# Gathered u rows for 32 of 384 dense tokens in a retrieval layer, with 68 chunks in the table stage

## The chip, the core and the metric

The kernel runs on one core of a Trainium2 chip. TensorE (PE in the profile, PEld its weight loads) multiplies matrices, VectorE (DVE) and ScalarE (ACT) work elementwise, GpSimd (POOL) issues the indirect DMAs that gather rows by index, and SyncE (SP) issues the other DMAs. Each engine runs its own instructions in the order in which they were placed, and engines wait for each other by semaphores. The metric is the device time of one execution in microseconds; less is better.

## What is computed

One encoder layer over 512 tokens of 1024 channels: a token mixer (sparse attention and pooling), then a retrieval over 16,384 single-neuron experts. Only the second half is touched:

```python
q = (hx @ w_q).reshape(TOKEN_BLOCK, PEER_HEADS, 2, PEER_HALF)
s = jnp.einsum('nhpd,hpkd->nhpk', q, sub_keys)
top_s, top_i = lax.top_k(s, PEER_TOPK)
cand = top_s[:, :, 0, :, None] + top_s[:, :, 1, None, :]
best_s, best_p = lax.top_k(cand.reshape(...), PEER_TOPK)
expert = (i1 * N_KEYS + i2).reshape(TOKEN_BLOCK, PEER_HEADS * PEER_TOPK)   # 128 per token
gate = softmax(best_s)
act = gelu(einsum('nd,ned->ne', hx, u[expert]))
return einsum('ne,ned->nd', gate * act, v[expert])
```

Each token picks 128 experts (8 heads, 16 each). Its activation with an expert is the dot product of the token with that expert's row of `u`, and the output is the sum of the experts' rows of `v`, each times gate and gelu of the activation.

## The kernel before

The 512 tokens go two ways. The last 128 are **sparse**: `sparse()` gathers, for k of 0 to 127, the row of `u` of each token's k-th expert into a 128x1024 tile (`ur`, one indirect DMA on POOL), VectorE multiplies it with the tokens (`hx`) and sums along the row (line 732, one instruction of 1024 elements a partition and a short one that reads the sum), and later the same is done with rows of `v` (`vr`, line 738, added into `sacc` in line 743).

The first 384 tokens (`ND`) are **dense**: all 16,384 experts are computed, in 128 chunks of 128 experts. A chunk has two parts. *Activations*: the 512 KB block `uT[c]` is loaded by `fetch` and split into a high and a low float32r part (ScalarE line 533 `uhe`, VectorE line 534 `ule`); 24 matmuls (8 slices of 128 channels, three products each, lines 570 to 572 or 554 to 556, tile `pse`) give 128 experts x 384 tokens, and ScalarE's gelu stores them (`gelu`). *Contraction*: the activations are multiplied by the gates of the chunk (`gated`, line 781), split again (`Wh`, `Wl`, lines 794, 796), a 512 KB block of `v` is loaded and split (`vh`, `vl`, lines 795, 797), and 18 matmuls of 512 columns (line 805, `acc`) add into six PSUM banks that stay for all 128 chunks.

The gates are wanted as a full table, experts x tokens, since most are zero. `gates(tb)` builds it for one block of 128 tokens: for every token two one-hot matrices (`on`, line 652: which second key; `oa`, line 658: which first key, times the gate, once for each of two float16 parts of the gate), and TensorE multiplies them (line 665, `gm`, two matmuls a token). ScalarE moves the result to `st`, and SP writes it to HBM (`gd`), from where the contraction reads it back in pieces (`g`).

Two stages follow from that:
- **Table stage.** While the tables are built and the keys of the next block are selected (`ProductKeys`), `dense_acts` computes activations of the first KEPT + SPILL = 37 + 22 = 59 chunks, KEPT of them held in SBUF, SPILL written to HBM (`ad`). Program order interleaves them: `act_until` advances the activations in step with the table (fractions `FILL`), and a scheduler then places each engine's instructions.
- **Contraction stage.** A loop over all 128 chunks, in an order written by hand for PE, DVE and ACT. An iteration c forms the weights of chunk c + 1 and the gated values of c + 2, takes some steps of `sparse()` (EARLY = 0.8 in the first SPILL iterations, RATE = 3.0 in those that still compute activations, and `late`, worked out so that all 256 are done 7 chunks before the end), then computes the activations of chunk c + KEPT (the last 69 chunks) or loads spilled ones, and contracts chunk c.

The buffers `up` (of the split `u`), `v`, `vh`, `vl`, `Wh`, `Wl` are two deep each, the gathered rows of `sparse()` five deep.

## Time and profile before

| | us |
|---|---|
| median of 3 runs (lowest, highest) | 1550.58 (1547.45, 1550.72) |
| profiled execution, its own time | 1549.25 |
| span of its instructions | 1547.4 |
| table stage: first dense activations to first `acc` matmul | 405 to 729.5 |
| contraction stage: first `acc` matmul to last | 729.5 to 1541.3 |
| last additions and the write of the output | to 1547.4 |

The time before 405 us (token mixer, query projection) has the same work in both kernels. A row of the timeline gives the start, then the duration of an instruction or of several merged (x2); instructions of one engine overlap by some ten ns, so that what one costs in a row of its kind is the difference of two starts, and that is used below.

### The profile page before, as it was taken

The numbers are of one execution on the slowest core, as the hardware profiler recorded it, in microseconds if no ns is written. First come the engines' busy times: TensorE is split into PE (matmuls) and PEld (weight loads), VectorE is DVE, ScalarE is ACT, GpSimd is POOL, SyncE is SP. The second block draws the span as 40 slices with busy tenths as digits, with TensorE's granted clock in tenths as the row PEclk, the third lists the DMA queues.
The fourth block names the chain that finished last, engine by engine and source line by source line (L and its number), as shares of the span: only waits on it lengthen the run. The fifth ranks groups of instructions, "written<-read, shape, count | busy, mean of one in ns | idle before, by whom it ended". The sixth has DMA issues, their size and how long they took to land.

```text
span 1547.4 us, 22248 instructions
## 1 busy us (share of the span) xinstructions
PE 1504.0 (97%) x7889; PEld 1302.0 (84%) x7889; DVE 1295.0 (84%) x2672; ACT 650.9 (42%) x999; POOL 324.9 (21%) x318
## 2 busy tenths in 40 slices
PE   5899999998999999999999999999999999999998
PEld 3678777886898989899888999999999999998886
DVE  7799886758999899994778888888888888888887
ACT  4643555534445454454334333333333333333332
POOL 0000000000000000001113444444444444453320
PEclk8999999999999999999999999999999999999999
DMA  8422663433236666779989999999999999998883
GB/s 313 163 69 83 213 221 116 157 112 121 78 113 189 193 198 183 224 244 319 330 316 365 323 352 357 318 363 315 359 343 337 355 320 361 328 355 315 314 305 145
DMA packets 158545, 393.91 MB, mean 255 GB/s; under 512 B 13537, under 2 KB 68449, under 8 KB 158306
## 3 DMA queue, kind: packets, MB, share of 16 engines
q1 hardware_dynamic: 121570, 258.26, 47.8%
q0 software_dynamic: 36864, 134.23, 24.5%
q8 instruction: 62, 1.02, 0.3%
q14 instruction: 49, 0.40, 0.1%
HBM read 358.75 MB, written 33.69 MB: 254 GB/s over the span
## 4 chain that ended last, share of the span: by engine, by line
PE 87%; DVE 8%; DMA 2%; ACT 2%; issue 1%; SPq 0%; ACTq 0%; DVEq 0%
PE acc L805 32%; PE pse L556 6%; PE pse L555 6%; PE pse L554 6%; PE pse L570 4%; PE pse L572 4%; PE pse L571 4%; PE gm L665 3%; PE po L469 1%; DVE ule L534 1%; PE psga L171 1%; PE psga L172 1%; PE psga L173 1%; PE pso L171 1%; PE psgp L171 1%; PE psgp L173 1%
## 5 line engine op out<-in xcount | busy, mean ns | idle before, releaser
L730 POOL DMA_INDIRECT ur<-u,ei x128 | 157.0, 1226 | 601.5 <-DMA ad<-gelu 365.5
L805 PE MATMUL acc<-vh,Wl 128*128 128x512 f32 x768 | 237.3, 390 | 0.0
L805 PE MATMUL acc<-vl,Wh 128*128 128x512 f32 x768 | 237.0, 389 | 0.3 <-DVE vl L797 0.3
L805 PE MATMUL acc<-vh,Wh 128*128 128x512 f32 x768 | 236.7, 389 | 0.0
L738 POOL DMA_INDIRECT vr<-v,ei x128 | 165.0, 1289 | 213.9 <-DVE sacc L743 185.2
L797 DVE TENSOR_TENSOR vl<-v,vh 128x1024 fp32r<-128x1024 f32 x128 | 156.8, 1225 | 57.7 <-ACT vh L795 57.4
L556 PE MATMUL pse<-h2h,ule 128*128 128x384 f32 x552 | 185.2, 336 | 0.1
L555 PE MATMUL pse<-h2l,uhe 128*128 128x384 f32 x552 | 184.7, 335 | 0.0
L554 PE MATMUL pse<-h2h,uhe 128*128 128x384 f32 x552 | 184.4, 334 | 0.0
L794 ACT ACTIVATE Wh<-gelu 128x384 fp32r<-128x384 f32 x106 | 55.6, 525 | 290.9 <-PE acc L805 187.9
L534 DVE TENSOR_TENSOR ule<-ue,uhe 128x1024 fp32r<-128x1024 f32 x128 | 155.9, 1218 | 17.8 <-ACT uhe L533 17.7
L805 PEld LDWEIGHTS acc<-vl,Wh 128*128 128x128 f32 x768 | 144.0, 188 | 30.8 <-DVE vl L797 0.9
L805 PEld LDWEIGHTS acc<-vh,Wl 128*128 128x128 f32 x768 | 144.2, 188 | 29.9
L570 PE MATMUL pse<-h2h,uhe 128*128 128x384 f32 x472 | 168.2, 356 | 0.0
L572 PE MATMUL pse<-h2h,ule 128*128 128x384 f32 x472 | 161.4, 342 | 5.1 <-DVE ule L534 5.1
L743 DVE SCALAR_TENSOR_TENSOR sacc<-vr,wt,sacc 128x1024 f32<-128x1024 f32 x127 | 162.8, 1282 | 2.6 <-DMA vr<-v,ei 0.2
L805 PEld LDWEIGHTS acc<-vh,Wh 128*128 128x128 f32 x768 | 143.2, 188 | 24.5
L533 ACT ACTIVATE uhe<-ue 128x1024 fp32r<-128x1024 f32 x128 | 134.6, 1051 | 60.7 <-PE pse L571 51.1
L571 PE MATMUL pse<-h2l,uhe 128*128 128x384 f32 x472 | 159.5, 338 | 0.0
L732 DVE SCALAR_TENSOR_TENSOR ur<-ur,hx 128x1024 f32<-128x1024 f32 x128 | 150.8, 1220 | 1.6 <-DMA ur<-u,ei 1.5
L795 ACT ACTIVATE vh<-v 128x1024 fp32r<-128x1024 f32 x128 | 135.9, 1061 | 10.0 <-DMA v<-v 9.5
L796 DVE TENSOR_TENSOR Wl<-gelu,Wh 128x384 fp32r<-128x384 f32 x106 | 59.2, 559 | 56.8 <-ACT Wh L794 56.6
(424 smaller groups left out, 2722.0 us busy)
## 6 DMA issues: line engine op xcount, KB each, us to landing
ue<-uT SPq DMA_DIRECT2D x128, 512.0 KB, 5.4
v<-v SPq DMA_DIRECT2D x128, 512.0 KB, 5.7
wada<-w_ada SPq DMA_DIRECT2D x48, 512.0 KB, 4.5
gd<-st SPq DMA_DIRECT2D x24, 1024.0 KB, 5.7
g<-gd SPq DMA_DIRECT2D x48, 512.0 KB, 7.5
ad<-gelu SPq DMA_DIRECT2D x22, 192.0 KB, 3.0
wgp<-w_in SPq DMA_DIRECT2D x8, 512.0 KB, 3.7
wga<-w_in SPq DMA_DIRECT2D x8, 512.0 KB, 3.9
```

Source lines behind the costliest of these rows:

```text
L534: V.tensor_tensor(lo, src, hi.bitcast(F32), op=ALU.subtract)
L554: T.matmul(p, hi[:, k, :], h2h[:, k, :n], start=(k == 0), stop=False)
L555: T.matmul(p, hi[:, k, :], h2l[:, k, :n], start=False, stop=False)
L556: T.matmul(p, lo[:, k, :], h2h[:, k, :n], start=False, stop=(k == DT - 1))
L570: T.matmul(ps, hi[:, k, :], h2h[:, k, :ND], start=(k == 0), stop=False)
L571: T.matmul(ps, hi[:, k, :], h2l[:, k, :ND], start=False, stop=False)
L572: T.matmul(ps, lo[:, k, :], h2h[:, k, :ND], start=False, stop=(k == DT - 1))
L730: G.indirect_dma_start(out=ur, out_offset=None, in_=u, in_offset=bass.IndirectOffsetOnAxis(ap=ei3[:, k:k + 1], axis=0))
L738: G.indirect_dma_start(out=vr, out_offset=None, in_=v, in_offset=bass.IndirectOffsetOnAxis(ap=ei3[:, k:k + 1], axis=0))
L743: V.scalar_tensor_tensor(sacc, vr, wt[:, k:k + 1], sacc, op0=ALU.mult, op1=ALU.add)
L797: V.tensor_tensor(vl, vr, vh.bitcast(F32), op=ALU.subtract)
L805: T.matmul(acc[tb][i], x[:, t], y[:, i * 512:(i + 1) * 512], start=(c == 0 and n == 0), stop=(c == NEXP - 1 and n == 2))
```

## The change

The first 32 of the dense tokens (`US`) no longer take their activations from the chunks. Their 128 experts each are gathered: 32 indirect DMAs of `u`, each of which serves 4 experts of 32 tokens (`UG` = 4 groups on the 128 partitions), each followed by one multiply-and-sum on VectorE (`gathers`). The gelu of these, times the gates, goes through the one-hot products in place of the gate alone (`values`, then `build`), in three bfloat16 parts, so the table holds finished weights for these 32 tokens, and the contraction takes them from the table (`first`).

The activation matmuls have 352 columns in place of 384. The table is built in four segments: tokens 32 to 127 of block 0, blocks 1 and 2, then tokens 0 to 31 of block 0, which must wait for all gathers. HOLD, SPILL, EARLY and RATE are set anew: the table stage has 35 + 33 = 68 chunks, the contraction stage 60, and `late` is 1.714 rows an iteration in place of 1.11.

```diff
-HOLD = 38
-SPILL = 22
+US = 32
+NU = ND - US
+UG = P // US
+HOLD = 36
+SPILL = 33
-EARLY = 0.8
+EARLY = 1.0
-RATE = 3.0
+RATE = 2.95
-FILL = (0.36, 0.72, 1.0)
+SEGS = [(0, US, P, 0.30, 0.4), (1, 0, P, 0.64, 0.4), (2, 0, P, 0.93, 0.4), (0, 0, US, 1.0, 0.0)]
...
-                T.matmul(ps, hi[:, k, :], h2h[:, k, :ND], start=(k == 0), stop=False)
+                T.matmul(ps, hi[:, k, :], h2h[:, k, US:ND], start=(k == 0), stop=False)
...
+        def values():
+            zero = oh.tile([P, P], F32, tag="gs", name="uz", bufs=1)
+            V.memset(zero, 0.0)
+            for i in range(UG):
+                r = slice(i * US, (i + 1) * US)
+                A.activation(zero[r, r], uact[r], AF.Gelu)
+            ps = ptr.tile([P, 4, P], F32, tag="tr", name="uw")[:, 0, :US]
+            T.matmul(ps, zero, con[:, K_SEL:K_SEL + US], start=True, stop=True)
+            V.tensor_tensor(ugate, ps, ugate, op=ALU.mult)
+            part = oh.tile([P, 3, US], BF16, tag="part", name="upart", bufs=1)
+            for i in range(3):
+                A.copy(part[:, i, :], ugate)
+                if i < 2:
+                    V.tensor_tensor(ugate, ugate, part[:, i, :], op=ALU.subtract)
+            yield from build(0, 0, US, ukeys, ulow, [part[:, i, :] for i in range(3)], BF16, 1.0)
...
-                    for i in range(2):
-                        x = oh.tile([P, NA, 4, KL, 2], F16, tag=f"oa{i}", name=f"oa{i}_{tb}_{t}")
+                    for i in range(len(parts)):
+                        x = oh.tile([P, NA, 4, KL, 2], dt, tag=f"oa{i % 2}", name=f"oa{i}_{tb}_{t}")
...
+        def gathers():
+            x = tokens(0, US, "u")
+            e = oh.tile([P, P], F32, tag="gs", name="ue", bufs=1)[:US]
+            V.scalar_tensor_tensor(e, sel[0][0][:US], 128.0, sel[0][1][:US], op0=ALU.mult, op1=ALU.add)
+            for i in range(UG):
+                V.tensor_copy(uei[i * US:(i + 1) * US, :], e[:, i * US:(i + 1) * US])
+            yield
+            for k in range(US):
+                ur = us.tile([P, D], F32, tag="row", name=f"uu{k}", bufs=2)
+                G.indirect_dma_start(out=ur, out_offset=None, in_=u,
+                                     in_offset=bass.IndirectOffsetOnAxis(ap=uei[:, k:k + 1], axis=0))
+                V.scalar_tensor_tensor(ur, ur, 1.0, x, op0=ALU.mult, op1=ALU.mult, accum_out=uact[:, k:k + 1])
+                yield
...
+        first = gts[c // GJ][:, :US // GT, c % GJ, :]
+        groups = lambda x: x[:, :US].rearrange("p (g t) -> p g t", t=GT)
+        A.activation(groups(wh), first, AF.Copy)
+        A.activation(wh[:, US:], w, AF.Copy)
         A.activation(vh, vr, AF.Copy)
-        V.tensor_tensor(wl, w, wh.bitcast(F32), op=ALU.subtract)
+        V.tensor_tensor(groups(wl), first, groups(wh).bitcast(F32), op=ALU.subtract)
+        V.tensor_tensor(wl[:, US:], w, wh[:, US:].bitcast(F32), op=ALU.subtract)
```

VectorE in the table stage, some three quarters through block 2 (`on`, `oa` are the one-hot tiles, `ule` the split of a chunk, `best`, `pos` and `cand` the selection of keys, `uu` a gathered row). Before:

```order
L652 TENSOR_TENSOR on_2_80_7039<-irep,keys_6426 128x1024
L658 TENSOR_TENSOR oa_2_80_7041<-gt_2_4_6915,rest_4_6911 128x1024
L658 TENSOR_TENSOR oa_2_80_7043<-gt_2_4_6917,rest_4_6911 128x1024
L908 TENSOR_TENSOR k_3h<-pr_7260 128x1024
L968 TENSOR_TENSOR sel_2_6576<-gate_7249,sm_7406 128x8x16
L908 TENSOR_TENSOR pr_7260<-k_3h 128x512
L652 TENSOR_TENSOR on_2_88_7093<-irep,keys_6426 128x1024
L534 TENSOR_TENSOR ule_7023<-ue_7021,uhe_7022 128x1024
```

After:

```order
L687 TENSOR_TENSOR oa_2_64_7061<-gt_2_4_7055,rest_4_7049 128x1024
L754 SCALAR_TENSOR_TENSOR uu_7073,uact<-uu_7073,hxu 128x1024
L537 TENSOR_TENSOR ule_7087<-ue_7085,uhe_7086 128x1024
L681 TENSOR_TENSOR on_2_72_7120<-irep,keys_6500 128x1024
L687 TENSOR_TENSOR oa_2_72_7122<-gt_2_4_7053,rest_4_7049 128x1024
L687 TENSOR_TENSOR oa_2_72_7124<-gt_2_4_7055,rest_4_7049 128x1024
L1007 MAX best_6831<-cand_6666 128x8 x2
L1008 MAX_INDEX pos_6832<-best_6831,cand_6666 128x8 x2
L1009 MATCH_REPLACE cand_6666<-best_6831,cand_6666 128x50 x2
L1010 MAX best_6831<-cand_6666 128x8 x2
L1011 MAX_INDEX pos_6832<-best_6831,cand_6666 128x8 x2
L754 SCALAR_TENSOR_TENSOR uu_7146,uact<-uu_7146,hxu 128x1024
```

The 32 multiplications of gathered rows stand on VectorE between the table's instructions, in line with the splits that TensorE's chunks need.

VectorE at the end of the table stage. Before, from the last one-hot product on:

```order
L658 TENSOR_TENSOR oa_2_120_7344<-gt_2_6_7155,rest_6_7149 128x1024
L908 TENSOR_TENSOR k_3h<-pr_7260 128x1024
L908 TENSOR_TENSOR pr_7260<-k_3h 128x512
L908 TENSOR_TENSOR pr_7260<-pr_7260 128x256
L908 TENSOR_TENSOR sel_1_6575<-pr_7260 128x128
L707 TENSOR_TENSOR hs<-h2h,h2l 128x1024
```

After, from the last but one group of tokens on:

```order
L681 TENSOR_TENSOR on_0_16_7775<-irep,ukeys 128x1024
L687 TENSOR_TENSOR oa_0_16_7777<-gt_0_0_7630,rest_0_7626 128x1024
L687 TENSOR_TENSOR oa_0_16_7779<-gt_0_0_7632,rest_0_7626 128x1024
L687 TENSOR_TENSOR oa_0_16_7781<-gt_0_0_7634,rest_0_7626 128x1024
L681 TENSOR_TENSOR on_0_24_7835<-irep,ukeys 128x1024
L687 TENSOR_TENSOR oa_0_24_7839<-gt_0_0_7632,rest_0_7626 128x1024
L537 TENSOR_TENSOR ule_7859<-ue_7857,uhe_7858 128x1024
L687 TENSOR_TENSOR oa_0_24_7837<-gt_0_0_7630,rest_0_7626 128x1024
L687 TENSOR_TENSOR oa_0_24_7841<-gt_0_0_7634,rest_0_7626 128x1024
L725 TENSOR_TENSOR hss<-h2h,h2l 128x1024
```

The last segment has three products for 8 tokens in place of two, and the selection for the fourth block (`k_3h`, `pr`, `sel`) is done ahead of it; 63 splits `ule` stand ahead of the last product, before 53.

VectorE late in the contraction stage, two iterations. Before:

```order
L743 SCALAR_TENSOR_TENSOR sacc<-vr_13849,wt,sacc 128x1024
L796 TENSOR_TENSOR Wl_13874<-gelu_11945,Wh_13873 128x384
L797 TENSOR_TENSOR vl_13872<-v_13870,vh_13871 128x1024
L781 TENSOR_TENSOR gelu_12016<-gelu_12016,g_13486 128x384
L743 SCALAR_TENSOR_TENSOR sacc<-vr_13882,wt,sacc 128x1024
L796 TENSOR_TENSOR Wl_13907<-gelu_12016,Wh_13906 128x384
L797 TENSOR_TENSOR vl_13905<-v_13903,vh_13904 128x1024
L781 TENSOR_TENSOR gelu_12088<-gelu_12088,g_13486 128x384
```

After:

```order
L872 TENSOR_TENSOR Wl_14214<-g_13853,Wh_14213 128x32
L873 TENSOR_TENSOR Wl_14214<-gelu_12191,Wh_14213 128x352
L874 TENSOR_TENSOR vl_14212<-v_14210,vh_14211 128x1024
L851 TENSOR_TENSOR gelu_12264<-gelu_12264,g_13853 128x352
L813 SCALAR_TENSOR_TENSOR sacc<-vr_14224,wt,sacc 128x1024
L813 SCALAR_TENSOR_TENSOR sacc<-vr_14227,wt,sacc 128x1024
L872 TENSOR_TENSOR Wl_14252<-g_13853,Wh_14251 128x32
L873 TENSOR_TENSOR Wl_14252<-gelu_12264,Wh_14251 128x352
L874 TENSOR_TENSOR vl_14250<-v_14248,vh_14249 128x1024
L851 TENSOR_TENSOR gelu_12335<-gelu_12335,g_13853 128x352
```

Five iterations of seven now add two gathered rows of `v`, before mostly one.

## Rows read from the trace of the kernel before

**Rows 1.** Chain that ended last: share of the span by engine.

```profile
PE 87%; DVE 8%; DMA 2%; ACT 2%; issue 1%; SPq 0%; ACTq 0%; DVEq 0%
```

**Rows 2.** Windows by stage: length, busy us (instructions) by engine, clock, DMA share, GB/s.

```profile
405.00:697.00 292.00, 282.11 (x2045) 262.98 (x2044) 281.23 (x973) 147.26 (x240) 0.00 (x0) 0.99 0.60 184
697.00:730.00 33.00, 32.97 (x201) 31.91 (x200) 15.51 (x21) 14.76 (x23) 3.17 (x3) 1.00 0.94 309
730.00:822.00 92.00, 91.59 (x405) 75.54 (x404) 65.34 (x95) 34.81 (x46) 16.41 (x17) 1.00 0.91 329
822.00:1388.00 566.00, 566.00 (x2881) 517.51 (x2880) 478.71 (x596) 202.86 (x275) 261.96 (x206) 1.00 0.94 343
1388.00:1520.00 132.00, 132.00 (x584) 109.31 (x583) 113.20 (x132) 48.43 (x64) 40.44 (x32) 1.00 0.83 297
```

**Rows 3.** Waits of VectorE, 405 to 697 us: total us, times, longest.

```profile
DVE ule L534 <- ACT uhe L533: 7.1, 8, 2.2
DVE top L893 <- ACT kss L890: 2.0, 4, 0.5
```

**Rows 4.** Timeline of TensorE, one contraction iteration: start, us, instruction.

```profile
902.89 0.34 PE L554 MATMUL pse<-h2h,uhe 128*128 128x384 f32 x1
...
907.06 0.61 PE L805 MATMUL acc<-vh,Wh 128*128 128x512 f32 x2
...
911.15 0.34 PE L554 MATMUL pse<-h2h,uhe 128*128 128x384 f32 x1
```

**Rows 5.** Timeline near 203 us, matmuls of 256 columns and the weight load behind.

```profile
202.76 0.28 PE L450 MATMUL lg<-k,qs 128*128 128x256 f32 x1
202.76 0.19 PEld L172 LDWEIGHTS psga<-hl,whga 128*128 128x128 f32 x1
202.88 0.39 PE L172 MATMUL psga<-hl,whga 128*128 128x512 f32 x1
```

**Rows 6.** Timeline of VectorE in the contraction stage: a split, then rows of u.

```profile
1104.08 1.22 DVE L534 TENSOR_TENSOR ule<-ue,uhe 128x1024 fp32r<-128x1024 f32 x1
1105.22 1.22 DVE L732 SCALAR_TENSOR_TENSOR ur<-ur,hx 128x1024 f32<-128x1024 f32 x1
...
1106.36 1.22 DVE L732 SCALAR_TENSOR_TENSOR ur<-ur,hx 128x1024 f32<-128x1024 f32 x1
```

**Rows 7.** Timeline of VectorE at the end of the table stage.

```profile
695.80 0.68 DVE L652 TENSOR_TENSOR on<-irep,keys 128x1024 f16<-128x1024 f16 x1
696.40 0.68 DVE L658 TENSOR_TENSOR oa<-gt,rest 128x1024 f16<-128x1024 f16 x1
697.01 0.68 DVE L908 TENSOR_TENSOR k_3h<-pr 128x1024 bf16<-128x1024 bf16 x1
...
698.84 1.23 DVE L707 TENSOR_TENSOR hs<-h2h,h2l 128x1024 f32<-128x1024 f32 x1
```

**Rows 8.** Timeline of TensorE at the first contraction.

```profile
729.52 0.61 PE L805 MATMUL acc<-vh,Wh 128*128 128x512 f32 x2
```

**Rows 9.** Groups of VectorE, 405 to 697 us: busy us, mean ns, idle before.

```profile
L658 DVE TENSOR_TENSOR oa<-gt,rest 128x1024 f16<-128x1024 f16 x96 | 62.3, 684 | 0.6 <-PE gm L665 0.5
```

**Rows 10.** Timeline of VectorE late in the contraction, an iteration with two rows.

```profile
1508.89 0.56 DVE L796 TENSOR_TENSOR Wl<-gelu,Wh 128x384 fp32r<-128x384 f32 x1 [0.20 <-ACT Wh L794]
1509.88 1.22 DVE L797 TENSOR_TENSOR vl<-v,vh 128x1024 fp32r<-128x1024 f32 x1 [0.43 <-ACT vh L795]
1511.02 0.55 DVE L781 TENSOR_TENSOR gelu<-gelu,g 128x384 f32<-128x384 f32 x1
1511.49 2.60 DVE L743 SCALAR_TENSOR_TENSOR sacc<-vr,wt,sacc 128x1024 f32<-128x1024 f32 x2
1514.01 0.55 DVE L796 TENSOR_TENSOR Wl<-gelu,Wh 128x384 fp32r<-128x384 f32 x1
```

**Rows 11.** Waits of all engines, 729 to 822 us: total us, times, longest.

```profile
ACT vh L795 <- DMA v<-v: 8.4, 9, 2.3
PEld acc L805 <- DVE vl L797: 0.7, 1, 0.7
```

**Rows 12.** DMA issues, 830 to 1090 us: count, median us to landing.

```profile
ur<-u,ei POOLq DMA_INDIRECT x94, 6.1
```

More of the change, by code (lines that the diff above doesn't have):

```diff
@@ L663, in gates @@
                             q, j = (t4 + k) // 2, k % 2
[L664 to L666 removed]
+                            for i, x in enumerate(gated):
+                                T.matmul(ps[:, k, :], two[:, q, :, j], x[:, :, q, :, j], start=(i == 0), stop=(i == len(gated) - 1))
+                        A.activation(st[:, :, t8 + t4:t8 + t4 + 4], ps.rearrange("p k e -> p e k"), AF.Copy, scale=scale)
                         yield
```

134 lines of the change are left out of this document (82 added, 52 removed).

## Prediction

> **What bounds the kernel now.** The chain of waits, read first, lies on TensorE for 87% of the span [rows 1], so a saving there looks like a saving of time. The windows by stage, read second, say where this is so [rows 2]. In the contraction stage (822 to 1388 us) TensorE is busy for 566 of 566 us and VectorE for 479; late in it (1388 to 1520) VectorE has 113 of 132. In the table stage (405 to 697) both are nearly full: TensorE 282, VectorE 281.2 of 292 us. Of the 10.8 us in which VectorE stands there, 7.1 are splits of a chunk that wait for ScalarE, and ScalarE in turn for buffers that TensorE still reads [rows 3]. Whatever is added to VectorE in the table stage therefore lengthens that stage, and whatever is taken from TensorE shortens the contraction stage alone. The change does both, and the question is which is larger.
>
> **TensorE: what a narrower matmul saves.** In a contraction iteration 24 matmuls of 384 columns take 907.06 - 902.89 = 4.17 us, 0.1738 each, and 18 of 512 columns 911.15 - 907.06 = 4.09, 0.2272 each [rows 4]. The difference of 128 columns costs 53.4 ns, 0.417 a column, so 32 columns fewer save 13.3 ns if nothing else sets the spacing. The weight load could: it is listed with 0.19 us. But a matmul of 256 columns was followed after 0.12 us by the next one with new weights, whose load of 0.19 us began with it [rows 5]; a spacing of 0.1604 us is thus above what loads force, and I take the 13.3 ns in full. A chunk's activations then take 24 x 0.1604 = 3.85 us.
>
> The Trainium skill (TensorE: Matmul & The Clock Gate, Back-to-back issue gap) gives another slope for streams of weight loads and matmuls: 81 ns at 128 columns and 131 ns at 512. By it 32 columns would be worth an estimated 4.2 ns. The rows speak against it, since 512 columns take 0.2272 us here; it stays as rival 3 below; by it the 60 chunks of the contraction stage would save an estimated 6 us in place of 19.2.
>
> **Contraction stage: what is removed.** It computes the activations of 60 chunks in place of 69: 9 x 4.17 = 37.5 us less, and the other 60 are each 24 x 13.3 ns shorter, 19.2 us. The 128 contractions stay. Together -56.7 us, if TensorE remains the bound.
>
> **Table stage: what is added on VectorE.** Splits and rows of 1024 elements cost 1.14 us, start to start (1104.08, 1105.22, 1106.36) [rows 6]; a one-hot product 0.60 (695.80, 696.40, 697.01) [rows 7], though its listed duration is 0.68 [rows 9].
> - 32 gathered rows: 32 x 1.14 = 36.5 us.
> - 63 splits ahead of the last product in place of 53, as the order shows: 10 x 1.14 = 11.4.
> - The third part of the gate: four products more, 2.4, and one of a quarter of that size, 0.2.
> - The transposed copy of the 32 tokens 1.2 (one like `hs`), some 16 small instructions on 32 columns 1.2 (an estimate, below a tenth of a us each, from the same row of 1024 elements at 1.14).
> - The selection that followed the last product (697.01 to 698.84 [rows 7]) now stands ahead of it: 1.8.
>
> That is 54.7 us. How much of VectorE's 10.8 us of standing remains has no row. The 7.1 us of waiting for splits should mostly go: TensorE needs 62 x 3.85 = 239 us for chunks where it had 53 x 4.17 = 221, with some 340 us for it. New waits come: in the last segment three products share the two buffers that TensorE must empty, and the gelu of the gathered sums goes through ScalarE and TensorE. Between nothing and 20 us I take 8, near the 10.8 of now. The last product then ends at 405 + 281.2 + 54.7 + 8 = 748.9, where it was 697.0.
>
> From there to the first contraction matmul it took 729.5 - 697.0 = 32.5 us [rows 7, 8], since TensorE was behind by eight chunks. In the new order 151 activation matmuls stand behind the last table matmuls, 24.2 us, with 1.3 for those and eight transposes: 25.5. The first contraction starts at 774.4, 44.9 later. The other chain there, table to HBM and back to the first gated values, ended with the first split weights before TensorE was free, and stays hidden; uncovered it would cost a few us.
>
> **Late contraction: VectorE becomes the bound.** An iteration with two gathered rows took 1514.01 - 1508.89 = 5.12 us on VectorE, of which 0.43 was a wait for ScalarE that goes when VectorE is late [rows 10]: 4.69. The new kernel adds a small split of 32 columns (0.09, estimated as above) and saves 64 columns (0.07): 4.71. The two rows took 2.52, so with one row it is 3.45. With 1.714 rows the mean is 3.45 + 0.714 x 1.26 = 4.35 us against TensorE's 4.09. Over 28 iterations that is 7.3 us; the buffers are two deep, and the split ends 2.1 us after the iteration's first instruction (1508.89 to 1511.02 [rows 10]), which leaves 2 us of advance. I take +5.5; bounds 0 (more advance) and 11. In the 60 iterations ahead of that, VectorE had 479 of 566 us at 3 rows an iteration; with 7.94 us for one instead of 8.26 it keeps room.
>
> **Early contraction: the DMAs.** An iteration loads 512 KB of `v`, 192 of gates, 192 of spilled activations and 0.8 x 512 of rows, 1.34 MB in 4.09 us or 327 GB/s, and the window shows 329 at a share of 0.91 [rows 2]. ScalarE waited there nine times for `v`, 8.4 us in total, and TensorE under 1 us [rows 11]. Now the rows are 1.0 and the spill 176 KB: 1.43 MB, 349 GB/s, for 33 iterations in place of 22. The middle stage sustained 343 GB/s at a share of 0.94 with TensorE never idle [rows 2], so this is just above what a row shows. I take +2, bounds 0 and 8.
>
> **Sum.** +44.9 - 56.7 + 5.5 + 2 = -4.3 us against the span of 1547.4: 1543.1, and 1545.0 for the profiled execution's own time. That execution was 1.3 us below the median of the three runs; on the median the forecast is 1546.3.
>
> **Rivals.**
> 1. *VectorE waits for gathered rows in the table stage; slower.* A gather takes about 1 us on GpSimd and 6.1 us to land [rows 12], and the third one needs the buffer of the first, so a row is ready 7.1 us after the last but one was used. On the mean two rows are 344 / 32 x 2 = 21.5 us apart, but at the end of block 2 the order has only some 8.5 us of work between them. It decides from 7.4 / 32 = 0.23 us of waiting for each row, where the forecast turns to slower by 0.2%. At 0.5 us each, 16 us: 1562. For it: the order on VectorE is fixed, and in this stage no gather ran before, so no row shows one beside the float16 products. Against it: the spacing. The Trainium skill (SBUF — State Buffer, SBUF: two separate sides) says that GpSimd cannot write descriptors while VectorE runs in a two-port mode; by it a gather's issue would wait out one such instruction, an estimated 0.6 us for a product, which the mean spacing hides. No run here shows it.
> 2. *The DMAs cannot feed the contraction stage.* Late, 1.714 rows are 1.62 MB an iteration, 396 GB/s at TensorE's pace. If a full share gives 343 / 0.94 = 365 GB/s [rows 2], an iteration takes 4.44 us: 10 us in place of 5.5; with 6 early in place of 2 it is 1555. Against it: gathers run five buffers ahead.
> 3. *The spacing of matmuls does not follow the columns.* The 19.2 us stay, and 2 at the end of the table stage: 1567. Against it are the two groups of rows above [rows 4, 5].
> 4. *VectorE is packed without gaps.* Standing falls from 8 to 2 and the late stage loses 1 in place of 5.5: 1536.
>
> **Chances.** Forecast 0.46, rival 1 0.20, rival 2 0.19, rival 3 0.05, rival 4 0.10. A measurement of this kernel tells 0.2%, 3.1 us, from no change: 1547.5 to 1553.7 is the same. The forecast's own spread, 1540 to 1553, lies for 0.34 below that and 0.12 in it. Rival 4 is faster; rival 1 0.17 slower and 0.03 the same; rival 2 0.03 faster, 0.07 the same, 0.09 slower; rival 3 slower. Faster 0.47, same 0.22, slower 0.31. Since cases of both signs matter, the likeliest one's own range stands here: 1540 to 1553. The range 1532 to 1564 holds it with rivals 2 and 4 and most of rival 1.
>
> **What would show it.** Right: activation matmuls 0.160 us apart; VectorE over 96% busy in a table stage whose first `acc` starts near 774; TensorE less busy there than before; iterations of 7.94 us from the 34th on; late ones near 4.3, with TensorE waiting for `vl` or `Wl`. Wrong: VectorE's waits in the table stage headed by the DMA of `uu` (rival 1); waits for `v` or gathered rows in the contraction (rival 2); a spacing of 0.17 (rival 3). If the table stage ends past 785, its standing was taken too small.

## The result: slower, and where the forecast lost it

The changed kernel takes 1592.77 us (median of 4, 1591.74 to 1593.85), the kernel before 1549.86 on the same chip: a ratio of 1.028, with a 95% interval of 1.0263 to 1.0296. The forecast was 1546.3 us with a range of 1532 to 1564, so the change went the other way, by 43 us. The profiled execution has a span of 1590.0 us, 46.9 more than the 1543.1 worked out for it.

The forecast was made stage by stage, and the trace gives each stage back. "Loss" is what the iterations take beyond 4.08 us (18 contraction matmuls without a stop):

| | before | forecast | after | after - forecast |
|---|---|---|---|---|
| VectorE at work, 405 us to the end of the last one-hot product | 281 | 335.9 | 335.7 | -0.2 |
| VectorE standing there | 10.8 | 8 | 27.9 | +19.9 |
| last product to first `acc` | 32.5 | 25.5 | 27.6 | +2.1 |
| **first `acc` matmul** | 729.5 | 774.4 | 796.25 | **+21.9** |
| loss of the first 32 iterations, and of the one behind them | 1 | 2 | 11.9 + 6.8 | +16.7 |
| 60 iterations with activations, each | 8.26 | 7.94 | 8.127 | +11.2 in all |
| loss of the last iterations | 0 | 5.5 | 4.2 | -1.3 |

The rest, -1.6, is mostly the rounding of the forecast's 4.09 for 4.08 and the end of the program. Three terms were mis-sized, all in the same direction: the table stage's standing, the early iterations, and the matmuls. The prediction's own sign for the first, a table stage that ends past 785, came true.

The chain of waits of the changed kernel, by engine. In [rows 1] TensorE had 87% and the DMAs 2%:

```profile
PE 59%; DVE 18%; DMA 15%; issue 4%; ACT 3%; POOL 0%; SPq 0%; ACTq 0%; DVEq 0%; POOLq 0%
```

The windows by stage, with the columns of [rows 2] (length, busy us of PE, PEld, DVE, ACT and POOL, clock, DMA share, GB/s): table stage to the last product, from there to the first `acc`, the first 32 iterations, the one behind them, then iterations with activations, then late ones:

```profile
405.00:768.00 363.00, 323.67 (x2313) 298.61 (x2311) 335.08 (x1069) 163.28 (x271) 42.85 (x32) 0.96 0.66 215
768.00:796.00 28.00, 27.37 (x186) 26.09 (x185) 11.83 (x18) 12.74 (x21) 0.44 (x1) 1.00 0.90 295
796.00:940.00 144.00, 136.76 (x585) 109.75 (x584) 104.68 (x185) 53.05 (x97) 36.27 (x34) 0.99 0.91 321
940.00:956.00 16.00, 12.28 (x49) 10.54 (x48) 10.38 (x18) 5.20 (x7) 4.50 (x4) 0.79 0.99 377
980.00:1400.00 420.00, 420.00 (x2174) 381.11 (x2173) 362.21 (x502) 155.28 (x260) 196.13 (x154) 1.00 0.93 345
1440.00:1560.00 120.00, 119.04 (x514) 95.35 (x513) 118.60 (x161) 46.21 (x85) 70.32 (x43) 1.00 0.95 360
```

VectorE has 335.08 of 363 us in the table stage, 92%, where the forecast wanted over 96%; the other 27.9 us it stands. Its waits up to the last product, ScalarE's for the loads of `uT`, and last the same wait of ScalarE in the kernel before (405 to 697 us; total us, times, longest):

```profile
DVE ule L537 <- ACT uhe L536: 20.5, 15, 5.5
DVE top L970 <- ACT kss L967: 3.7, 3, 2.0
DVE uu L754 <- DMA uu<-u,uei: 3.5, 2, 3.1
...
ACT uhe L536 <- DMA ue<-uT: 50.0, 17, 7.3
...
ACT uhe L533 <- DMA ue<-uT: 5.1, 2, 3.8
```

In [rows 3] VectorE waited 7.1 us for `uhe`, which the prediction put down to buffers that TensorE still read; ScalarE waited 5.1 us for loads of `uT`, in two waits. Now it waits 50.0 us for them. The gathered rows themselves (`uu`) cost VectorE 3.5 us: waiting for them was rival 1, and that is not where the time went. The longest of these stops, in the timeline (SP's rows are issues of DMAs; in brackets the idle time before, and what ended it):

```profile
680.41 3.00 SPq L581 DMA_DIRECT2D ad<-gelu  x1
683.50 1.09 SPq L543 DMA_DIRECT2D ue<-uT  x1
...
691.70 1.06 ACT L536 ACTIVATE uhe<-ue 128x1024 fp32r<-128x1024 f32 x1 [7.26 <-DMA ue<-uT]
...
692.78 1.23 DVE L537 TENSOR_TENSOR ule<-ue,uhe 128x1024 fp32r<-128x1024 f32 x1 [5.45 <-ACT uhe L536]
...
692.81 0.43 PE L570 MATMUL pse<-h2h,uhe 128*128 128x352 f32 x1 [3.92 <-ACT uhe L536]
```

The write of a spilled activation holds SyncE's queue for 3.0 us, the load behind it goes out at 683.50 and has landed at 691.70, and ScalarE, VectorE and TensorE stand one behind the other. VectorE's one-hot products stand behind this split in its queue. Two suspects, then: the queue, or the way of the load.

In the contraction an iteration is 8.13 us, the activations 4.00 (forecast 3.85), the contraction 4.13 (before 4.09 [rows 4]), by the timeline of TensorE:

```profile
1099.92 0.63 PE L882 MATMUL acc<-vh,Wh 128*128 128x512 f32 x2
...
1104.05 0.33 PE L554 MATMUL pse<-h2h,uhe 128*128 128x352 f32 x1
1104.22 0.33 PE L555 MATMUL pse<-h2l,uhe 128*128 128x352 f32 x1
...
1108.05 0.63 PE L882 MATMUL acc<-vh,Wh 128*128 128x512 f32 x2
```

### The profile page after: what moved, and what is told of

It is laid out like the page before. It is cut to its first block, busy times and chain, and to the rows that moved or that the text cites. A ratio compares the mean times of both kernels' runs of the same rounds, so it can differ in the third digit from the quotient of the medians.

```text
span 1590.0 us, 22784 instructions
## 1 busy us (share of the span) xinstructions
PE 1504.3 (95%) x7931; PEld 1285.4 (81%) x7931; DVE 1341.7 (84%) x2883; ACT 662.1 (42%) x1138; POOL 380.7 (24%) x350
## 4 chain that ended last, share of the span: by engine, by line
PE 59%; DVE 18%; DMA 15%; issue 4%; ACT 3%; POOL 0%; SPq 0%; ACTq 0%; DVEq 0%; POOLq 0%
PE acc L882 18%; DMA ue<-uT 5%; DMA v<-v 5%; PE pse L556 5%; PE pse L554 5%; PE pse L555 5%; DVE ule L537 3%; DMA vr<-v,ei 3%; DVE vl L874 2%; PE pse L572 1%; PE po L473 1%; PE pse L570 1%; PE pse L571 1%; DVE oa L687 1%; PE gm L694 1%
## 5 line engine op out<-in xcount | busy, mean ns | idle before, releaser
L882 PE MATMUL acc<-vl,Wh 128*128 128x512 f32 x768 | 240.2, 393 | 3.1 <-DVE vl L874 3.0
L808 POOL DMA_INDIRECT vr<-v,ei x128 | 180.3, 1409 | 160.5 <-DVE sacc L813 115.2
L570 PE MATMUL pse<-h2h,uhe 128*128 128x352 f32 x544 | 184.8, 340 | 11.7 <-ACT gelu L579 6.4
L572 PE MATMUL pse<-h2h,ule 128*128 128x352 f32 x544 | 184.2, 340 | 7.2 <-DVE ule L537 7.1
L571 PE MATMUL pse<-h2l,uhe 128*128 128x352 f32 x544 | 181.8, 334 | 0.0
L882 PEld LDWEIGHTS acc<-vl,Wh 128*128 128x128 f32 x768 | 143.2, 188 | 40.3 <-DVE vl L874 10.2
L869 ACT ACTIVATE Wh<-g 128x32 fp32r<-128x32 f32 x128 | 29.3, 229 | 319.4 <-PE acc L882 308.8
L554 PE MATMUL pse<-h2h,uhe 128*128 128x352 f32 x480 | 158.5, 330 | 3.0 <-ACT uhe L536 3.0
L556 PE MATMUL pse<-h2h,ule 128*128 128x352 f32 x480 | 158.1, 329 | 0.7 <-DVE ule L537 0.7
L555 PE MATMUL pse<-h2l,uhe 128*128 128x352 f32 x480 | 158.3, 330 | 0.0
L802 DVE SCALAR_TENSOR_TENSOR ur<-ur,hxs 128x1024 f32<-128x1024 f32 x128 | 151.3, 1218 | 0.4 <-DMA ur<-u,ei 0.4
L570 PEld LDWEIGHTS pse<-h2h,uhe 128*128 128x128 f32 x544 | 105.4, 194 | 14.9 <-ACT gelu L579 7.9
```

Source lines behind the costliest of these rows:

```text
L554: T.matmul(p, hi[:, k, :], h2h[:, k, t], start=(k == 0), stop=False)
L555: T.matmul(p, hi[:, k, :], h2l[:, k, t], start=False, stop=False)
L556: T.matmul(p, lo[:, k, :], h2h[:, k, t], start=False, stop=(k == DT - 1))
L570: T.matmul(ps, hi[:, k, :], h2h[:, k, US:ND], start=(k == 0), stop=False)
L571: T.matmul(ps, hi[:, k, :], h2l[:, k, US:ND], start=False, stop=False)
L572: T.matmul(ps, lo[:, k, :], h2h[:, k, US:ND], start=False, stop=(k == DT - 1))
```

## Experiments: the table stage

First `acc` and VectorE's standing up to the last product, of all runs in this group:

| kernel | standing | first `acc` | time |
|---|---|---|---|
| changed | 27.9 | 796.25 | 1592.8 |
| `norows`: no gathers there | 9.7 | 779.8 | 1568.7 |
| `actq`: spill written by ScalarE | 25.6 | 795.1 | 1584.5 |
| `deep`: three buffers for `uT` | 5.5 | 772.6 | 1554.4 |
| `deepdouble`: each row multiplied twice | 8.0 | 814.5 | 1593.6 |
| `deepnomults`: rows only read | 42.3 | 781.5 | 1561.5 |

Standing is the span from 405 us to the end of the last product less VectorE's busy time, as in the windows. The expectations were written with 29 us for the changed kernel's 27.9. The last two rows are one execution each.

**Without the gathers.**

```diff
-                G.indirect_dma_start(out=ur, out_offset=None, in_=u,
-                                     in_offset=bass.IndirectOffsetOnAxis(ap=uei[:, k:k + 1], axis=0))
-                V.scalar_tensor_tensor(ur, ur, 1.0, x, ...)
+                V.scalar_tensor_tensor(ur, x, 1.0, x, ...)
```

> The changed kernel without the 32 gathers of the table stage: VectorE multiplies the tokens with themselves in place of a gathered row, so its work stays, and the activations of the 32 tokens are left out. Theory that the gathers' transfers delay the loads of uT: VectorE's standing up to the last one-hot product falls from 29 us to about 10, the first contraction starts near 776 in place of 796, the time falls by some 20 us to 1573. Rival (the loads are late because SyncE's queue stands at the writes of spilled activations): standing stays above 22 us, the first contraction at 790 or later, the time falls by less than 6 us.

The standing fell to 9.7 us, the first `acc` to 779.8, the time to 1568.7. VectorE's work was the same, by the window up to the last product, and so was the order of SyncE's queue:

```profile
405.00:749.00 344.00, 315.27 (x2311) 290.86 (x2310) 334.26 (x1068) 162.44 (x271) 0.00 (x0) 0.98 0.57 178
```

So the gathers make VectorE stand, though it hardly waits for the gathered rows. From the trace's records of landings: nine of ten loads of `uT` land within 6.2 us of their issue in the kernel before, 6.5 without the gathers, and 7.9 in the changed kernel. Of the 24 us, 16.4 are gone by the first `acc`; the rest is in the early iterations, which are told of below.

**The queue.**

```diff
-                nc.sync.dma_start(out=ad[c - KEPT], in_=g)
+                nc.scalar.dma_start(out=ad[c - KEPT], in_=g)
```

> The changed kernel with one edit: the writes of spilled activations are issued by ScalarE behind their gelu, and no longer stand in SyncE's queue. Theory that this queue delays the loads of uT: the 33 us between a free buffer and the issue of its load fall below 5, VectorE's standing up to the last product from 29 us to 10 to 15, the first contraction starts at 778 to 783, the time falls by 12 to 18 us to about 1578. Rival (transfers of gathers, or VectorE's own order): the issue delays fall and the loads land as late as now; the time changes by less than 5 us.

Between a free buffer and the issue of its load there were 32 us in all, and 12 now; but VectorE still stands for 25.6 us, and the loads now land later (9 in 10 within 8.4 us). The rival was right for this stage: SyncE's queue is not the main cause. Nor does the run without the gathers point at it: 21 us of such delay were left there, with 9.7 us of standing. The Trainium skill (DMA: Bandwidth & Descriptors, Issuing engines are not separate DMA queues) says that DMAs issued from several engines run on the same DMA engines, so that another issuer saves only issue time; the trace agrees, with 20 us less delay of issues and 2.3 us less standing. Of the 8.3 us that this run gains, some 6 lie in the early iterations, which lost 5.7 in place of 11.9; that loss differs between kernels that share these iterations (below).

**A third buffer.**

```diff
-HOLD = 36
-SPILL = 33
+HOLD = 33
+SPILL = 36
...
-        w = up.tile([P, DT, P], F32, tag="u", name=f"u{name}")
+        w = up.tile([P, DT, P], F32, tag="u", name=f"u{name}", bufs=3)
...
-            vr = up.tile([P, DT, P], F32, tag="u", name=f"v{c}").rearrange("p k e -> p (k e)")
+            vr = up.tile([P, DT, P], F32, tag="u", name=f"v{c}", bufs=3).rearrange("p k e -> p (k e)")
```

The second edit follows from the first: late in the contraction every second block of `v` uses the same buffers.

> The changed kernel with three buffers in place of two for the loads of uT; SBUF has room for that with 32 kept and 36 spilled chunks in place of 35 and 33. Theory (with two buffers each load is waited for over its whole way from the issue to the landing, 6 to 8 us, and the gathers made this way longer): VectorE's standing up to the last one-hot product falls from 29 us to 8 to 15, the first contraction starts at 776 to 784, the time falls by 8 to 18 us although 3 more chunks are read back in the early iterations. Rival (the DMAs lack rate, not time): standing stays at 25 us or more, the time rises by 0 to 5 us with the further spill.

It did more than the 8 to 18 us expected: 1554.4 us, 38 us less than the changed kernel and 0.3% above the kernel before (ratio 1.0027, 1.0011 to 1.0043). ScalarE no longer waits for a load of `uT` at all, and VectorE stands for 5.5 us. Its waits up to the last product:

```profile
DVE uu L754 <- DMA uu<-u,uei: 2.6, 3, 1.9
DVE top L970 <- ACT kss L967: 2.6, 2, 2.1
DVE ule L537 <- ACT uhe L536: 0.2, 1, 0.2
```

Its window up to there:

```profile
405.00:743.00 338.00, 312.73 (x2303) 288.16 (x2302) 332.54 (x1067) 160.82 (x268) 45.37 (x32) 0.98 0.73 232
```

VectorE is 98% busy, and the first `acc` is at 772.6, where the forecast had put it (774.4). The loads land as late as in the changed kernel (9 in 10 within 8.0 us), only a buffer earlier. With two buffers a load is issued when the split of the last but one chunk is done (within 0.03 us at the median); the way of the load, ScalarE's split of 1.06 us and VectorE's of 1.22 then fit into the time of two chunks or not. In the changed kernel two chunks have 11.7 us on the mean (62 loads in 363 us), and 7.9 + 2.3 us are close to that. That the one-hot products, which stand between the splits, use up what is left is argued and not measured. Between the two spans lie 40.9 us: 23.7 up to the first `acc`, 12 from TensorE's spacing (other buffers have moved, see below: not the third buffer's own work), 11.4 in the early iterations, and 6.0 given back by the late ones, which have 1.8 rows each here.

**Does VectorE's work count in full?** Once by doubling it, once by taking it away, both on the kernel with three buffers.

```diff
                 V.scalar_tensor_tensor(ur, ur, 1.0, x, ..., accum_out=uact[:, k:k + 1])
+                V.scalar_tensor_tensor(ur, ur, 1.0, x, ..., accum_out=spare)
```

> The kernel with three buffers for uT, in which each of the 32 gathered rows is multiplied twice on VectorE, 32 x 1.14 = 36.5 us more there; the second sum is not used. Theory (VectorE bounds the table stage once the loads are covered): the first contraction moves from 772.6 to 805 to 812, VectorE's standing stays below 12 us. Rival (what was put on VectorE was partly hidden, since TensorE is nearly as long there): 797 or earlier.

Some 38 us more work on VectorE moved the first `acc` by 41.9 us, to 814.5, a little past the range; the standing grew by 2.5 us, to 8.0, and the stretch behind the last product by 1.5. The theory holds: with the loads covered, each us on VectorE in this stage is at least a us of time.

```diff
-                V.scalar_tensor_tensor(ur, ur, 1.0, x, ..., accum_out=uact[:, k:k + 1])
+                V.tensor_copy(uact[:, k:k + 1], ur[:, 0:1])
```

> The kernel with three buffers for uT, in which VectorE reads one column of each gathered row (below 0.1 us) in place of multiplying the row (1.14 us): 32 x 1.05 = 33.6 us less on VectorE in the table stage; the activations of the 32 tokens are left out. Theory (VectorE bounds that stage, so each us on it counts in full): the first contraction, at 772.3 there, starts at 736 to 744. Rival (TensorE with 68 chunks, 313 of 338 us busy, is the next bound close behind): 755 or later, with VectorE standing over 20 us.

This run tells nothing on the question: the scheduler put the short reads of the rows close behind each other, and VectorE stood for the gathers. Its longest wait up to 749 us:

```profile
DVE uact L754 <- DMA uu<-u,uei: 31.4, 10, 7.7
```

It shows rival 1 at work, though: a row that is asked for sooner than its gather lands is waited for. In the changed kernel, where other work stands between the multiplications, VectorE waited for two rows.

## Experiments: the early iterations

The forecast gave them 2 us of loss. They lost 11.9, and the first iteration with activations 6.8. The stops come where the loads of `v` are late. In [rows 11] ScalarE waited nine times for `v`, 8.4 us in 92; here, in the 144 us of the first 32 iterations:

```profile
ACT vh L871 <- DMA v<-v: 27.0, 17, 4.1
...
PE acc L882 <- ACT vh L871: 5.1, 4, 1.8
```

The timeline of the first iteration with activations:

```profile
943.67 1.06 ACT L871 ACTIVATE vh<-v 128x1024 fp32r<-128x1024 f32 x1 [3.92 <-DMA v<-v]
944.88 1.06 ACT L536 ACTIVATE uhe<-ue 128x1024 fp32r<-128x1024 f32 x1 [0.15 <-DMA ue<-uT]
...
945.99 0.64 PE L554 MATMUL pse<-h2h,uhe 128*128 128x352 f32 x1 [3.03 <-ACT uhe L536]
...
948.07 0.49 PE L554 MATMUL pse<-h2h,uhe 128*128 128x352 f32 x1
948.36 0.49 PE L555 MATMUL pse<-h2l,uhe 128*128 128x352 f32 x1
```

And the window around its first matmuls, with the granted clock as the third number from the end:

```profile
946.00:949.00 3.00, 2.31 (x7) 1.86 (x8) 3.00 (x6) 1.79 (x4) 0.03 (x1) 0.51 1.00 399
```

TensorE stands 3.0 us and 0.7 more, and then its matmuls are 0.29 us apart in place of 0.167, at a granted clock of 0.51 (1.2 of 2.4 GHz): the stops are 3.7 of the 6.8 us, and the rest, about half, is the clock.

**Fewer rows of `u`.**

```diff
-EARLY = 1.0
+EARLY = 0.8
...
-RATE = 2.95
+RATE = 3.1
```

> The changed kernel with EARLY = 0.8 in place of 1.0 rows of u in each of the first 33 iterations, and RATE = 3.1 in place of 2.95 in the next 60, so that the late iterations keep theirs. Theory (the early iterations ask more than the DMAs give): their 11.9 us over 4.08 each fall below 4, the 6.8 us of the first iteration with activations below 3, the rest as now: 8 to 12 us less, 1581 to 1585. Rival (the stalls come with the reading of gates, every eighth iteration, whatever the rows): 11.9 us fall by less than 4, and the time by less than 4 us.

1578.4 us: 14 less. The loss fell to 3.3 us, that of the first iteration with activations to 4.1, and that of the late iterations from 4.2 to 0.8, since they have 1.63 rows in place of 1.71. The table stage stayed (795.35).

```diff
-EARLY = 1.0
+EARLY = 0.0
```

> The changed kernel with EARLY = 0: no row of u is gathered in the first 33 iterations, and the late iterations take 2.89 rows each in place of 1.71, which makes them longer; what is read here are the early iterations. Theory (the rows ask too much of the DMAs there): the 11.9 us over 4.08 each fall below 1.5, and the first iteration with activations from 14.9 below 10 us. Rival (the gates read every eighth iteration stall them by themselves): 6 us or more remain, at the iterations 3, 9, 17 and 25.

Without rows 2.1 us are left (expected below 1.5), all at the start, and the first iteration with activations takes 8.5 us. So the rows are what costs the early iterations their time, and not the gates, which are read as before. The windows of these iterations, the last two numbers being DMA share and GB/s. Without rows:

```profile
796.00:930.00 134.00, 132.51 (x584) 109.07 (x583) 75.10 (x128) 50.77 (x97) 4.32 (x4) 1.00 0.74 244
```

With 0.8:

```profile
795.00:930.00 135.00, 133.22 (x584) 108.80 (x583) 99.19 (x174) 51.75 (x96) 27.72 (x28) 1.00 0.91 320
```

At 1.0 rows this stage is at an edge: kernels with the same early iterations lost 11.9 (changed), 11.2 (`pad3968`), 10.7 (`pad128`), 9.1 (`starts`), 7.6 (`full384`), 5.7 (`actq`) and 4.1 us (`norows`). What of that is due to the edits and what to chance these runs don't tell, and the 3.3 us at 0.8 rows lie close to the lowest of them. With three buffers for `uT` and 36 such iterations, 0.8 rows were no better than 1.0: 6.9 and 4.3 us (`best`, `bestq`, below) for 6.4 (`deep`). The loss is small for certain only at 0.6 rows (1.1, `best6`) and at none (2.1).

## Experiments: the matmul's spacing

The changed kernel has 0.1667 us for 352 columns where the forecast had 0.1604. Is it a floor, set by something other than the columns?

**Other widths in the kernel before.**

```diff
+            n = WIDTHS[c % 8] if 0 < k < DT - 1 else ND
+            T.matmul(ps[:, :n], hi[:, k, :], h2h[:, k, :n], ...)
```

> The kernel before, in which 18 of the 24 activation matmuls of each contraction chunk (the slices 1 to 6) have 384, 376, 368, 360, 352, 336, 320 or 256 columns by turns, so that for part of the tokens the activations lack these slices. Theory (a floor under the spacing): 384 columns 0.1738 us apart, 376 0.170, and all from 368 down to 256 at 0.1667, the spacing that the changed kernel shows at 352. Rival (the slope of 0.417 ns a column goes on, and 0.1667 at 352 has another cause, such as where the columns begin): 352 at 0.160, 320 at 0.147, 256 at 0.120.

Mean spacing within the 18 varied matmuls of a chunk, ns:

| columns | 384 | 376 | 368 | 360 | 352 | 336 | 320 | 256 |
|---|---|---|---|---|---|---|---|---|
| spacing | 173.6 | 173.1 | 166.6 | 164.4 | 160.7 | 153.3 | 146.2 | 119.2 |

The theory of a floor is refuted, and the rival was right: some 0.42 ns a column down to 256, with 352 at 160.7, as forecast. The spacing does not fall evenly, though: 376 columns take nearly what 384 do, and 368 take 6.5 ns less. The first of 18 matmuls of 320 and of 256 columns, and the first one behind them:

```profile
908.95 0.31 PE L557 MATMUL pse<-h2h,uhe 128*128 128x320 f32 x1
...
911.58 0.34 PE L557 MATMUL pse<-h2h,uhe 128*128 128x384 f32 x1
...
916.77 0.28 PE L557 MATMUL pse<-h2h,uhe 128*128 128x256 f32 x1
...
918.92 0.34 PE L557 MATMUL pse<-h2h,uhe 128*128 128x384 f32 x1
```

That is 2.63 / 18 = 0.146 and 2.15 / 18 = 0.119. The Trainium skill (TensorE: Matmul & The Clock Gate, Back-to-back issue gap) has 81 ns at 128 columns and 131 at 512 for such streams; these runs don't agree, with 119 at 256 and 227 at 512.

**Other first columns in the changed kernel.**

```diff
+    PLACES = ((0, 32, 352), (0, 0, 352), (32, 32, 352), (0, 0, 384), (0, 16, 352), (0, 64, 352), (0, 32, 256), (0, 0, 256))
```

> The changed kernel, in which 18 of the 24 activation matmuls of each contraction chunk read other columns: 352 from column 32 (as it is), 352 from 0, 352 from 32 written to columns from 32, 384 from 0, 352 from 16, 352 from 64, 256 from 32 and 256 from 0, by turns; the activations of the dense tokens lack parts by that. In the kernel before, 352 columns from 0 were 0.1607 us apart; in the changed kernel 352 from 32 are 0.1667. Theory (the first column matters): 0.1667 for those from column 32, 0.1607 for 352 from 0, 0.120 for 256 from 0 and more for 256 from 32. Rival (something else in the changed kernel, such as the place of its tiles or the work beside): 352 columns at 0.1667 wherever they begin, also from 0.

352 columns from 32: 166.6 ns, whether written to 0 or to 32; from 0 160.7, from 16 160.1, from 64 160.7; 256 columns from 32 118.9 and from 0 119.2; 384 173.4. So, of the forms tried, the slow spacing belongs to the 352 columns from 32 alone, the form that the change uses; 256 columns from 32 are not slow, against the theory. 18 of them, and 18 from column 0, in the timeline:

```profile
1037.88 0.33 PE L558 MATMUL pse<-h2h,uhe 128*128 128x352 f32 x1
...
1040.88 0.33 PE L558 MATMUL pse<-h2h,uhe 128*128 128x384 f32 x1
...
1046.06 0.32 PE L558 MATMUL pse<-h2h,uhe 128*128 128x352 f32 x1
...
1048.96 0.34 PE L558 MATMUL pse<-h2h,uhe 128*128 128x384 f32 x1
```

But the kernel with three buffers has the same columns from 32 at 0.1587. There `h2h` and the split `uT`, which these matmuls read, stand where they stood; the buffers of the contraction (`v`, `vh`, `vl`, `Wh`, `Wl`) stand 4224 bytes lower.

**The place of the contraction's buffers.**

```diff
+    shift = ctx.enter_context(tc.tile_pool(name="shift", bufs=1, reuse_waits="tile")).tile([P, 32], F32, name="shift")
     vp = ctx.enter_context(tc.tile_pool(name="vp", bufs=2, reuse_waits="tile"))
```

> The changed kernel with an unused tile of 128 bytes a partition ahead of the buffers of v, vh, vl, Wh and Wl, which moves these by 128 bytes; h2h and the split uT stay where they are. Theory (the place of the contraction's operands decides in which of two patterns TensorE runs; with 128 bytes more they stand modulo 512 as in the kernel before): contraction matmuls 226.6 us / 1000 apart as there, in place of 229.2, activation matmuls 0.160 in place of 0.1667, an iteration of 7.93 us. Rival (the place doesn't matter): 0.2292, 0.1667 and 8.127 us.

> The changed kernel with an unused tile of 3968 bytes a partition there, which puts the same buffers modulo 8192 where they stand in the kernel with three buffers for uT. Theory (their place decides): an iteration of 7.926 us with activation matmuls 0.1587 apart, as in that kernel. Rival (what decides is something else that the three buffers change): 0.1667 and 8.127 us.

Both gave an iteration of 7.926 us, with activation matmuls 0.1587 apart and the contraction's at 0.2280 in place of 0.2292, and 1576.4 and 1579.1 us (one execution each): 14 to 16 us less for an unused tile, of which 12 are these iterations. An iteration of the kernel with 128 bytes more, 7.92 us from one first `pse` to the next:

```profile
1103.72 0.32 PE L554 MATMUL pse<-h2h,uhe 128*128 128x352 f32 x1
1103.88 0.33 PE L555 MATMUL pse<-h2l,uhe 128*128 128x352 f32 x1
...
1107.53 0.62 PE L883 MATMUL acc<-vh,Wh 128*128 128x512 f32 x2
...
1111.64 0.32 PE L554 MATMUL pse<-h2h,uhe 128*128 128x352 f32 x1
```

The place of these buffers decides it in this stage. Not in the way that was expected: the contraction matmuls did not go back to the 226.6 ns of the kernel before, and both shifts gave the same pattern. It is not the place alone either. In the table stage of the changed kernel, where none of these buffers is read, both spacings occur: 15 steps of 0.1667 (683.72 to 686.22), and 11 of 0.158 (773.99 to 775.73):

```profile
683.72 0.33 PE L570 MATMUL pse<-h2h,uhe 128*128 128x352 f32 x1
...
686.22 0.33 PE L570 MATMUL pse<-h2h,uhe 128*128 128x352 f32 x1
...
773.99 0.32 PE L570 MATMUL pse<-h2h,uhe 128*128 128x352 f32 x1
...
775.73 0.32 PE L572 MATMUL pse<-h2h,ule 128*128 128x352 f32 x1
```

So the same stream of weight loads and matmuls has one of two spacings and keeps it over a stretch of matmuls. In the contraction stage the place of the buffers and the first column bear on which. Why is open.

**What the narrower matmul gave.**

```diff
-                A.activation(gelus[a], multiply(pending.pop(a), slice(US, ND), f"e{a}"), AF.Gelu)
+                A.activation(gelus[a], multiply(pending.pop(a), slice(0, ND), f"e{a}")[:, US:], AF.Gelu)
```

> The changed kernel with 384 columns again in the activation matmuls of the 60 contraction chunks (the 32 further columns are not used); the table stage as it is. Theory (a start at column 32 costs 6 ns a matmul): 24 matmuls take 4.17 us as in the kernel before, an iteration 8.25 us in place of 8.127, and the contraction is 60 x 0.125 = 7.5 us longer: 1600. Rival (the narrower matmul saves the 13.3 ns of the forecast, and something else in the changed kernel slows all matmuls by 6 ns): an iteration of 8.44 us, 19 us longer: 1612.

An iteration of 8.30 us, between the two: 0.173 x 60 = 10.4 us, of the 19.2 that the forecast had counted. The time rose by 3.7 us only, to 1596.5, since the early iterations lost less in this run (7.6 us, and 6.4 in the first one with activations). The 384 columns are at 0.1733 and the contraction's at 0.2295: with this place of the buffers the contraction is slower at either width. It is so only between activations: in the iterations without them, before and behind, 18 of its matmuls take 4.08 us in the changed kernel too.

## Experiments: what would be faster

**Only the chunks moved**, at 384 columns and without gathers (`SPILL = 31` in the kernel before), and the same with three buffers (`HOLD = 35`, `SPILL = 34`, `RATE = 3.2`):

> The kernel before with 31 spilled chunks in place of 22, so that 68 chunks are computed in the table stage and 60 later, as in the changed kernel, at 384 columns and with no gathered rows there. Theory (9 chunks cost the table stage 10 us of VectorE and some standing, the contraction saves 37.5 us, and the early iterations, now 31 long, lose 5 to 15 us waiting for DMAs): first contraction at 745 to 755, time 1532 to 1545, less than before. Rival (the table stage loses as much as the contraction gains): first contraction at 765 or later, time 1550 or more.

> The kernel before with 68 chunks in the table stage (34 kept, 34 spilled), three buffers for uT and RATE = 3.2: what is left of the best kernel without gathered rows and with 384 columns. Theory (with 384 columns TensorE becomes the bound of the table stage: in the run with 68 chunks and two buffers VectorE waited 15 us for it): first contraction at 757 or later, time 1546 to 1556, so the gathered rows and the narrower matmuls are what the best kernel gains by. Rival (moving the chunks is the whole gain): first contraction at 750 or earlier, 1540 or less.

The first gave 1557.3 us (ratio 1.0033, 1.0019 to 1.0047) with a first `acc` at 764.3: close to the rival's case, with 8.7 us lost in the late iterations besides, which have 1.77 rows each there. The second gave 1549.2 (0.9991, 0.9981 to 1.0) with 766.6 and no late loss, as its theory had it: no gain over the kernel before. With 384 columns TensorE is the bound of the table stage: 313 of 322 us in the window of `moved`, and VectorE waits for it to empty the one-hot products (total us, times, longest):

```profile
DVE oa L658 <- PE gm L665: 15.0, 8, 3.0
```

```profile
405.00:727.00 322.00, 313.12 (x2226) 295.29 (x2226) 294.38 (x989) 158.85 (x255) 0.00 (x0) 0.99 0.62 185
```

A third buffer doesn't help there (14.7 us). What the gathered rows and the narrower matmuls bring is seen against the best kernel below, which also has 68 chunks and three buffers: its table stage is 6.7 us longer (first `acc` at 773.3), and its early and late iterations lose some 4 us more, but 60 iterations of 7.93 in place of 8.26 us give 20 back. They pay in the contraction, not in the table stage.

**The third buffer alone** in the kernel before (`HOLD = 35`, `SPILL = 25`, 59 chunks):

> The kernel before with three buffers for uT (34 kept and 25 spilled chunks, 59 together as now). Theory that the third buffer answers the gathers and the 68 chunks of the change: here VectorE stands 12 us in the table stage, of which a third buffer can take back at most 10, while 3 more spilled chunks cost 0 to 5: 1543 to 1552. Rival (the third buffer helps any kernel of this form as much as it helped the changed one, 38 us): below 1535.

1551.4 us, a ratio of 1.0006 (0.9995 to 1.0016): nothing gained, as the 5.1 us of waiting for `uT` there had suggested.

**All together**: three buffers, `EARLY = 0.8`, `RATE = 3.2`; then fewer early rows, and the other queue:

> The changed kernel with three buffers for uT (32 kept and 36 spilled chunks), EARLY = 0.8 and RATE = 3.2 together. From the run with three buffers (1554.4 us) the early iterations should lose 3 us in place of 6.4, and the late ones, with 1.49 rows in place of 1.8, none in place of 10.2: about 1542, less than the kernel before by 0.5%. Rival (the DMAs only wait elsewhere: with 3.2 rows the middle iterations, 93% DMA share at 2.95, become the bound): middle iterations above 8.0 us in place of 7.93, 1550 or more.

> The kernel with three buffers, EARLY = 0.8 and RATE = 3.2 (1539.2 us), with EARLY = 0.6 and RATE = 3.3. Theory (rows of u slow the early iterations): their 6.9 us over 4.08 each fall to 2 to 4, the middle ones stay at 7.93 us although the DMA share is 0.98 already, and the time falls by 2 to 5 us. Rival (the middle iterations have no room for more rows): above 7.97 us, no gain or a loss.

> The same kernel (three buffers, EARLY = 0.8, RATE = 3.2: 1539.2 us) with the writes of spilled activations issued by ScalarE. Theory (with three buffers the loads of uT have time enough, so that SyncE's queue costs nothing more): within 4 us of 1539. Rival (the queue still delays something, by the 7 us that the same edit gave the changed kernel): 1533 or less.

The first gave 1539.25 us (1536.66 to 1543.61), a ratio of 0.9931 (0.9916 to 0.9947) to the kernel before: 10 us faster than before and 53 faster than the change as it was made. First `acc` at 773.3, early loss 6.9, iterations of 7.927, late loss 1.3. The early iterations did not get better, against the expectation (3 us for 6.4); what the new pace gives back lies in the late ones (1.3 for 10.2). The other two kernels don't improve on it: 1543.1 (0.9952) and 1541.1 (0.9939). With 0.6 rows the early loss is 1.1, but the middle iterations go to 7.966 and the late loss to 3.1: the rows that leave one stage load another, and the middle one is at a DMA share of 0.98, as a window of `best` shows:

```profile
950.00:1420.00 470.00, 469.43 (x2471) 424.02 (x2470) 424.57 (x583) 176.72 (x297) 259.47 (x189) 1.00 0.98 372
```

## Why the prediction was wrong, step by step

- **VectorE's added work: right.** 54.7 us were counted; work rose from 281.3 to 335.7, by 54.4. That it counts in full once the loads are covered is shown (`deepdouble`).
- **Standing in the table stage: the step that failed first.** The forecast took 8 us, near the 10.8 of now, out of bounds of 0 to 20; it was 27.9, past the upper one. It looked at what VectorE had waited for, TensorE's buffers, and saw that go. It did not ask what the loads of `uT` needed: two buffers, so that each load has less than two chunks' time from its issue to its split, with 16.8 MB of gathers new beside them. ScalarE's wait for these loads went from 5.1 to 50.0 us. That the gathers cause it is shown by `norows` (9.7 us of standing), that a third buffer covers it by `deep` (5.5 us, with the gathers in place and the loads as slow); SyncE's queue as the main cause is refuted by `actq`.
- **Rival 1** had the right place and the wrong mechanism: VectorE waits 3.5 us for gathered rows, and over 20 for the loads that the gathers delay. Its price for that, 16 us, was close to the 16.4 that `norows` gave back in this stage.
- **First `acc` behind the last product: right within 2.1 us,** 27.6 for 25.5. TensorE stands for 0.6 us there, so the loads are not what this stretch waits for.
- **Early iterations: mis-sized.** 349 GB/s were set against 343 from a middle stage, with a loss of 2 and at most 8. It was 18.7. The middle stage was the wrong row to compare with: even 320 GB/s are not carried without loss here (`early08`, 3.3 us in 32 iterations), and the middle carries 372 in `best` at 7.93 us an iteration. That the shorter period is the reason, 4.08 us with two buffers for `v`, is argued; no run gave `v` a third buffer here. Rival 2 had this mechanism, with 6 us.
- **Matmul spacing: right as a slope, wrong for this kernel.** 352 columns do take 0.1607 us in the kernel before (`widths`), and 0.1587 after a shift of 128 bytes. In the changed kernel they took 0.1667, and the contraction's matmuls 1% more: 11.2 us. The rows that the forecast used gave one spacing for a width, and it took that for the only one.
- **Late iterations: right.** 4.2 us for 5.5, with VectorE 118.6 of 120 us busy and TensorE waiting for `vl`, as forecast; an iteration with two rows takes 4.63 us (forecast 4.71), by its timeline:

```profile
1518.82 0.19 DVE L872 TENSOR_TENSOR Wl<-g,Wh 128x32 fp32r<-128x32 f32 x1
...
1523.45 0.18 DVE L872 TENSOR_TENSOR Wl<-g,Wh 128x32 fp32r<-128x32 f32 x1
```

The sum of the forecast was a small difference of large terms, -56.7 and +44.9. Each of the three misses (19.9, 16.7 and 11.2 us) was larger than the -4.3 that was left.

## What to carry to other kernels

When an engine's queue gets work with transfers of its own, look at the loads that run beside it, not only at the new ones: ask how many are in flight, and whether issue, landing and the first use still fit into the time that their buffers give. A DMA rate that one stage carries need not be carried by another: here 372 GB/s cost nothing at 7.93 us an iteration, and 320 cost 3.3 us at 4.08. And where a buffer is cheap, try a third before giving up a change: here it turned 2.8% slower into 0.3%, and with the rows paced anew into 0.7% faster. Read the stages before giving it all the credit: of the 41 us, 12 came from where other buffers happened to move, which an unused tile gave as well.
